# HGRN scores from 32 stationary columns at a time, with masked copies once per head

## The chip, the cores and the metric

The kernel runs on one core of one Trainium2 chip. The metric is the device time of one execution in microseconds, and the time of a kernel is the median of its timed runs. Before the change three runs took 2264.58, 2264.91 and 2265.63 us, so the time before is 2264.91 us.

## The reference, cut to what matters

One decoder layer over 1024 tokens of width 1024, all in float32: a combined input projection, an HGRN2 branch and a retention branch, gates, an output projection and an MLP. The change touches only the scores of the HGRN2 branch, which has 8 heads with 128 keys each:

```python
b = jnp.cumsum(lfc, axis=2)                                   # log of the forget gates
rel = jnp.where(causal, b[:, :, :, None, :] - b[:, :, None, :, :], -jnp.inf)
scores = jnp.einsum('bhid,bhijd,bhjd->bhij', qc, jnp.exp(rel), kc)
o = (jnp.einsum('bhij,bhje->bhie', scores, vc)
     + jnp.einsum('bhid,bhde->bhie', qc * jnp.exp(b), state))
```

The score of query i and key j in a chunk carries, for each of the 128 key channels, the product of the forget gates between j and i. It is not one matrix product. The reference uses chunks of 64 tokens; the result does not depend on their length, and the kernel uses chunks of 128, so a head has 8 chunks.

## The kernel before, in words

The projections and the MLP are dense products of three float32r passes each (`mm3`, lines 188 to 190; the products into the PSUM tiles `psd` are most of them). The HGRN branch lies in the middle of the program. `h_stream` walks over the heads in steps, 9 per head: a step gives one piece of `h_levels` (the scores of head h) and one of `h_states` (the recurrence over the chunks of head h - 1), and `mix` puts dense products (`h_fill`, later `r_first`) between the steps. A scheduler then fixes the order of each engine's instructions when the kernel is built. Every engine runs its own in that order.

`h_levels` makes the scores by doubling. On the first level, tokens stand in pairs (lines 850 to 858). Then `H_SIZES` gives three levels, blocks of 2, 8 and 32 tokens, and each joins four blocks into one of four times the size. Before a level, VectorE (DVE) multiplies the queries `X` and keys `k` by the gates that lie between (lines 880 and 881 before the products, 909, 910, 920 and 921 after them). Then for each of the 8 chunks one product is made whose stationary operand is all 128 keys of the chunk and whose moving operand is 192 query columns (line 891, line 854 on the first level): 128 x 192 results, two chunks to a PSUM bank `psa`. Only those in which key and query lie in the same group of four blocks mean anything. DVE picks them out with `copy_predicated` and byte masks, three copies to a bank (line 906; two on the first level, lines 857 and 858), into the score tile `S` (`hS`, named U in the trace). For the last two heads, ScalarE (ACT) copies the level of 32 in place of DVE (line 899). Float32 products run as two passes, so each is two weight loads and two matmuls in the trace. There are two `psa` buffers.

`h_states` then multiplies `S` by the values (line 957), the decayed queries by the state (956), and the keys by the values (962); it also transposes keys (939) and results (990).

Of the kernel before, what the change touches and what calls it, by code (L numbers as in the profile page):

```python
# [19 lines left out]
P = 128  # L20
# [27 lines left out]
N_MASK = P + 64 + 3 * 384  # L48
# [16 lines left out]
def constants():  # L65
# [15 lines left out]
    m[:, :P] = np.eye(P, dtype=np.float32)  # L81
    r = np.arange(64)[None, :]
    m[:, P:P + 64] = (j % 2 == 0) & (j // 2 == r)
    for n, s in enumerate(H_SIZES):
        half, quad = j // s % 4, j // (4 * s) == r // (2 * s)
        for i, f in enumerate((r // s % 2 * 2, 1, 0)):
            o = P + 64 + 384 * n + 128 * i
            m[:, o:o + 64] = m[:, o + 64:o + 128] = (half == f) & quad
# [46 lines left out]
class Trunk:  # L135
# [703 lines left out]
    def h_levels(self, p, hd):  # L839
# [4 lines left out]
        S = [self.hS[(2 * h + hf) % len(self.hS)] for hf in (0, 1)]  # L844
# [5 lines left out]
        for bk in range(4):  # L850
            pa = self.ps("a", (P, 384)).rearrange("p (c b w) -> p c b w", c=2, w=3)
            for c in (0, 1):
                n = 2 * bk + c
                nc.tensor.matmul(pa[:, c].rearrange("p b w -> p w b"), k[:, n * P:(n + 1) * P], q[:, :, n * 64:(n + 1) * 64], start=True, stop=True)
            Sv = S[bk // 2][:, bk % 2 * 2:bk % 2 * 2 + 2, :].rearrange("p c (b two) -> p c b two", two=2)
            mk = self.mask8[:, :P].rearrange("p (b two) -> p b two", two=2).unsqueeze(1).to_broadcast([P, 2, 64, 2])
            V.copy_predicated(Sv, mk, pa[:, :, :, 0:2])
            V.copy_predicated(Sv[:, :, :, 1], self.mask8[:, P:P + 64].unsqueeze(1).to_broadcast([P, 2, 64]), pa[:, :, :, 2])
            if bk == 1:
                yield  # L860
# [10 lines left out]
        for ln, sz in enumerate(H_SIZES):  # L871
# [14 lines left out]
            for bk in range(4):  # L886
                pa = self.ps("a", (P, 384))
                for c in (0, 1):
                    n = 2 * bk + c
                    mv = X[:, :, n * P:(n + 1) * P].rearrange("p w (b r) -> p b w r", r=4 * sz)[:, :, :, sz:]  # L890
                    nc.tensor.matmul(pa[:, c * 192:(c + 1) * 192].rearrange("p (b w r) -> p b w r", w=2, r=3 * sz),  # L891
                                     k[:, n * P:(n + 1) * P], mv, start=True, stop=True)
                pv = pa.rearrange("p (b w r s) -> p b w r s", w=2, r=3, s=sz)
                Sv = S[bk // 2][:, bk % 2 * 2:bk % 2 * 2 + 2, :].rearrange("p c (b f s) -> p (c b) f s", f=4, s=sz)
                if sz == 32 and p == 3:
                    qv = pv.rearrange("p b w r s -> p b (w r) s")
                    for r0, dst, src in ((0, slice(1, 2), slice(0, 1)), (64, slice(3, 4), slice(2, 3)), (32, slice(2, 4), slice(1, 5, 3)),
                                         (0, slice(2, 4), slice(3, 6, 2))):
                        nc.scalar.activation(Sv[r0:r0 + 32, :, dst], qv[r0:r0 + 32, :, src], AF.Copy)
                    if bk == 1:  # L900
                        yield
                    continue
                for j, (dst, src) in enumerate(((Sv[:, :, 1::2], pv[:, :, 0, 0::2]), (Sv[:, :, 2:4], pv[:, :, :, 1]),
                                                (Sv[:, :, 2:4], pv[:, :, 1, 0::2]))):
                    o = P + 64 + 384 * ln + 128 * j
                    V.copy_predicated(dst, self.mask8[:, o:o + 128].rearrange("p (b two s) -> p b two s", two=2, s=sz), src)
                if bk == 1:
                    yield
# [932 lines left out]
```

## Time and profile before

| what | value |
|---|---|
| median of 3 runs | 2264.91 us |
| profiled execution, its own time | 2266.02 us |
| its span | 2264.2 us |
| TensorE (PE) busy | 98% of the span, 10343 matmuls |
| DVE, ACT, POOL busy | 73%, 45%, 13% |
| first to last score product (lines 854, 891) | 891.5 to 1180.4 us |

PE is the weight loads (PEld) and the matmuls of TensorE; they overlap. A group's row gives busy time, the mean of one in ns and the idle time before it. Matmuls are pipelined: their recorded lengths overlap, so the time from one start to the next is what one costs in a stream. A row of the timeline holds a run of like instructions: its start, its length to the end of the last, and their count.

### The profile page before, as it was taken

The numbers are of one execution on the slowest core, as the hardware profiler recorded it, in microseconds if no ns is written. First come the engines' busy times: TensorE is split into PE (matmuls) and PEld (weight loads), VectorE is DVE, ScalarE is ACT, GpSimd is POOL, SyncE is SP. The second block draws the span as 40 slices with busy tenths as digits, with TensorE's granted clock in tenths as the row PEclk, the third lists the DMA queues.
The fourth block names the chain that finished last, engine by engine and source line by source line (L and its number), as shares of the span: only waits on it lengthen the run. The fifth ranks groups of instructions, "written<-read, shape, count | busy, mean of one in ns | idle before, by whom it ended". The sixth has DMA issues, their size and how long they took to land.

```text
span 2264.2 us, 29883 instructions
## 1 busy us (share of the span) xinstructions
PE 2227.3 (98%) x10343; PEld 1846.9 (82%) x10343; DVE 1645.1 (73%) x3035; ACT 1027.0 (45%) x1889; POOL 299.7 (13%) x469
## 2 busy tenths in 40 slices
PE   7999999999999999999999999999999999999998
PEld 5888888888888887888887888888878888888886
DVE  7866768786777647888875666777796666667778
ACT  4533334543333445343456555222575555643441
POOL 0111111111110112000011222022112222100001
PEclk9999999999999999999999999999999999999999
DMA  9766755543333446121235666864244444777863
GB/s 268 237 220 232 240 184 178 172 144 113 107 114 106 135 172 228 38 85 66 70 127 201 221 215 217 289 213 149 96 162 157 154 154 154 277 267 245 259 217 117
DMA packets 229144, 396.14 MB, mean 175 GB/s; under 512 B 17768, under 2 KB 122976, under 8 KB 228224
## 3 DMA queue, kind: packets, MB, share of 16 engines
q1 hardware_dynamic: 198240, 294.34, 40.5%
q0 software_dynamic: 30576, 99.82, 11.8%
q8 instruction: 82, 1.34, 0.2%
q14 instruction: 70, 0.57, 0.1%
q10 hardware_dynamic: 176, 0.06, 0.0%
HBM read 289.28 MB, written 104.87 MB: 174 GB/s over the span
## 4 chain that ended last, share of the span: by engine, by line
PE 92%; DVE 2%; DMA 2%; issue 2%; ACT 1%; POOL 1%; SPq 0%; DVEq 0%; ACTq 0%; POOLq 0%
PE psd L188 17%; PE psd L189 17%; PE psd L190 17%; PE psa L188 5%; PE psa L189 5%; PE psa L190 5%; PE psc L189 3%; PE psc L188 3%; PE psc L190 3%; PE psa L891 2%; PE psb L1213 2%; PE psb L188 2%; PE psb L189 2%; PE psb L190 2%; PE psc L1199 1%
## 5 line engine op out<-in xcount | busy, mean ns | idle before, releaser
L188 PE MATMUL psd<-U,wh 128*128 128x512 f32 x696 | 280.5, 405 | 1.0 <-ACT U L183 0.9
L189 PE MATMUL psd<-U,wh 128*128 128x512 f32 x696 | 278.4, 400 | 0.5 <-DVE U L184 0.4
L190 PE MATMUL psd<-U,wl 128*128 128x512 f32 x696 | 277.0, 398 | 0.0
L183 ACT ACTIVATE bh<-s 128x512 fp32r<-128x512 f32 x212 | 133.3, 633 | 255.8 <-PE psd L189 65.7
L188 PE MATMUL psd<-U,bh 128*128 128x512 f32 x528 | 205.5, 389 | 1.2 <-DVE e L450 1.2
L189 PE MATMUL psd<-U,bh 128*128 128x512 f32 x528 | 205.6, 389 | 0.1
L190 PE MATMUL psd<-U,bl 128*128 128x512 f32 x528 | 205.5, 389 | 0.0
L183 ACT ACTIVATE bh<-raw 128x512 fp32r<-128x512 f32 x159 | 101.0, 637 | 223.4 <-PE psd L189 92.4
L184 DVE TENSOR_TENSOR bl<-raw,bh 128x512 fp32r<-128x512 f32 x159 | 108.6, 690 | 122.7 <-ACT bh L183 122.3
L184 DVE TENSOR_TENSOR bl<-s,bh 128x512 fp32r<-128x512 f32 x212 | 145.0, 688 | 63.8 <-ACT bh L183 63.7
L189 PEld LDWEIGHTS psd<-U,wh 128*128 128x128 f32 x696 | 132.1, 190 | 26.6 <-DVE U L184 2.7
L188 PEld LDWEIGHTS psd<-U,wh 128*128 128x128 f32 x696 | 131.3, 190 | 27.0 <-ACT U L183 3.4
L190 PEld LDWEIGHTS psd<-U,wl 128*128 128x128 f32 x696 | 131.8, 189 | 25.3
L183 ACT ACTIVATE U<-hr 128x512 fp32r<-128x512 f32 x112 | 70.4, 630 | 143.3 <-issue 71.1
L188 PEld LDWEIGHTS psd<-U,bh 128*128 128x128 f32 x528 | 99.1, 188 | 22.6 <-DVE e L450 2.0
L189 PEld LDWEIGHTS psd<-U,bh 128*128 128x128 f32 x528 | 99.1, 188 | 21.1 <-DVE U L184 0.5
L190 PEld LDWEIGHTS psd<-U,bl 128*128 128x128 f32 x528 | 99.1, 188 | 20.4
L184 DVE TENSOR_TENSOR U<-hr,U 128x512 fp32r<-128x512 f32 x112 | 77.2, 689 | 49.6 <-ACT U L183 49.4
L183 ACT ACTIVATE wh<-raw 128x512 fp32r<-128x512 f32 (+1 forms) x79 | 57.0, 741 | 117.3 <-PE psd L189 88.5
L188 PE MATMUL psa<-U,bh 128*128 128x512 f32 x264 | 103.0, 390 | 1.6 <-ACT e L438 1.6
L190 PE MATMUL psa<-U,bl 128*128 128x512 f32 x264 | 102.7, 389 | 0.0
L189 PE MATMUL psa<-U,bh 128*128 128x512 f32 x264 | 102.7, 389 | 0.0
(447 smaller groups left out, 5593.3 us busy)
## 6 DMA issues: line engine op xcount, KB each, us to landing
raw<-in_w_in SPq DMA_DIRECT2D x146, 512.0 KB
raw<-in_w_down SPq DMA_DIRECT2D x64, 512.0 KB
raw<-in_w_ada SPq DMA_DIRECT2D x32, 512.0 KB
raw<-in_w_up SPq DMA_DIRECT2D x32, 512.0 KB
raw<-in_w_pb SPq DMA_DIRECT2D x20, 512.0 KB
adw<-in_w_ada SPq DMA_DIRECT2D x16, 512.0 KB
v_d<-e POOLq DMA_DIRECT2D x32, 256.0 KB, 4.1
rg_d<-e POOLq DMA_DIRECT2D x32, 256.0 KB, 2.6
```

Of the source, the lines that this page charges most:

```text
L183: self.nc.scalar.activation(hi, src, AF.Copy)
L184: self.nc.vector.tensor_tensor(lo, src, hi.bitcast(F32), op=ALU.subtract)
L188: r = mm(out, wh, uh, start=start, stop=False, skip_group_check=more)
L189: mm(out, wh, ul, start=False, stop=False, skip_group_check=more)
L190: return r, mm(out, wl, uh, start=False, stop=stop, skip_group_check=more)
L891: nc.tensor.matmul(pa[:, c * 192:(c + 1) * 192].rearrange("p (b w r) -> p b w r", w=2, r=3 * sz), k[:, n * P:(n + 1) * P], mv, start=True, ...
L1199: mm(G[e], l[:, n % 2, es], r, start=n == 0 and i == 0, stop=i == 2, skip_group_check=n > 0)
L1213: mm(po, l, r, start=i == 0, stop=i == len(pairs) - 1)
```

## The change

Each chunk's keys are taken in four groups of 32, and each group is multiplied only with the queries of its own 32 tokens. The product of group r goes to PSUM partitions 32r to 32r + 31, at the same columns as the other three. A chunk then gives 4 products of 32 stationary and 48 moving columns for each of the first three levels, in place of one of 128 and 192. The results of all 8 chunks fit in one PSUM bank of 128 x 384, so there are two masked copies on the first level and three on the levels of 2 and 8, per head. They go to a compact tile `hC` of 128 x 256 in which partition 32r + j holds the 32 x 32 diagonal block of key group r for every chunk.

On the level of 32 nothing need be masked, for the four blocks are the four groups. A chunk has four products, of 32, 64, 32 and 64 moving columns. ACT copies the results from two banks straight into `S` (6 copies per head) and then the four diagonal blocks out of `hC` (4 copies), for every head, so line 906's copies of that level go. `S` becomes one tile per head with all 8 chunks, two in turn. The masks are smaller, `rs` shares a tile with `ms`, and a level's products come in one step and not in two.

In numbers of the program: 256 score products become 1024, which in the trace are 512 and 2048 weight loads with as many matmuls. DVE's masked copies fall from 328 to 64. ACT's copies for the scores rise from 32 to 80.

The diff:

```diff
-N_MASK = P + 64 + 3 * 384
+N_MASK = 3 * P + 2 * 384
...
-        S = [self.hS[(2 * h + hf) % len(self.hS)] for hf in (0, 1)]
+        S, C = self.hS[h % 2], self.hC
...
-        for bk in range(4):
-            pa = self.ps("a", (P, 384)).rearrange("p (c b w) -> p c b w", c=2, w=3)
-            for c in (0, 1):
-                n = 2 * bk + c
-                nc.tensor.matmul(pa[:, c].rearrange("p b w -> p w b"), k[:, n * P:(n + 1) * P], q[:, :, n * 64:(n + 1) * 64], start=True, stop=True)
-            ...
-            V.copy_predicated(Sv, mk, pa[:, :, :, 0:2])
-            V.copy_predicated(Sv[:, :, :, 1], self.mask8[:, P:P + 64].unsqueeze(1).to_broadcast([P, 2, 64]), pa[:, :, :, 2])
-            if bk == 1:
-                yield
+        def blocks():
+            pa = self.ps("a", (P, 384))
+            for n in range(8):
+                for r in range(4):
+                    yield n, r, k[:, n * P + 32 * r:n * P + 32 * r + 32], pa[32 * r:32 * r + 32, 48 * n:48 * n + 48], pa
+
+        for n, r, kb, po, pa in blocks():
+            o = n * 64 + 16 * r
+            nc.tensor.matmul(po.rearrange("p (b w) -> p w b", w=3), kb, q[:, :, o:o + 16], start=True, stop=True)
+        pv = pa.rearrange("p (b w) -> p b w", w=3)
+        Cv = C.rearrange("p (b two) -> p b two", two=2)
+        V.copy_predicated(Cv, self.mask8[:, :2 * P].rearrange("p (b two) -> p b two", two=2), pv[:, :, 0:2])
+        V.copy_predicated(Cv[:, :, 1], self.mask8[:, 2 * P:3 * P], pv[:, :, 2])
+        yield
...
-            for bk in range(4):
-                pa = self.ps("a", (P, 384))
-                for c in (0, 1):
-                    ...
-                    nc.tensor.matmul(pa[:, c * 192:(c + 1) * 192].rearrange("p (b w r) -> p b w r", w=2, r=3 * sz),
-                                     k[:, n * P:(n + 1) * P], mv, start=True, stop=True)
-                ...
-                    V.copy_predicated(dst, self.mask8[:, o:o + 128].rearrange("p (b two s) -> p b two s", two=2, s=sz), src)
-                if bk == 1:
-                    yield
+            if last:
+                for hf in (0, 1):
+                    pa = self.ps("a", (P, 384)).rearrange("p (c i) -> p c i", c=4)
+                    for c in range(4):
+                        o = (4 * hf + c) * P
+                        Xc = X[:, :, o:o + P].rearrange("p w (f s) -> p w f s", s=sz)
+                        for r, col, mv in ((0, 0, Xc[:, 0, 1]), (1, 0, Xc[:, :, 2]), (2, 0, Xc[:, 0, 3]), (0, 32, Xc[:, 1, 1::2])):
+                            w = 32 if len(mv.shape) == 2 else 64
+                            po = pa[32 * r:32 * r + 32, c, col:col + w]
+                            nc.tensor.matmul(po if w == 32 else po.rearrange("p (w s) -> p w s", w=2),
+                                             k[:, o + 32 * r:o + 32 * r + 32], mv, start=True, stop=True)
+                    for r in range(3):
+                        w = 96 - 32 * r
+                        nc.scalar.activation(S[32 * r:32 * r + 32, 4 * hf:4 * hf + 4, P - w:], pa[32 * r:32 * r + 32, :, :w], AF.Copy)
+                for r in range(4):
+                    rs = slice(32 * r, 32 * r + 32)
+                    nc.scalar.activation(S[rs, :, rs], C[rs].rearrange("p (c i) -> p c i", c=8), AF.Copy)
+            else:
+                for n, r, kb, po, pa in blocks():
+                    o = n * P + 32 * r
+                    mv = X[:, :, o:o + 32].rearrange("p w (b r) -> p b w r", r=4 * sz)[:, :, :, sz:]
+                    nc.tensor.matmul(po.rearrange("p (b w r) -> p b w r", w=2, r=3 * sz), kb, mv, start=True, stop=True)
+                ...
+                    V.copy_predicated(dst, self.mask8[:, o:o + P].rearrange("p (b two s) -> p b two s", two=2, s=sz), src)
+            yield
...
-                nc.tensor.matmul(po, S[hf][:, c, :], vn, start=n == 0, stop=True)
+                nc.tensor.matmul(po, S[:, n, :], vn, start=n == 0, stop=True)
...
-        k.hS = [X[:, j].rearrange("p (c i) -> p c i", c=4) for j in range(4)]
-        for t in k.hS:
+        k.hS = [X[:, 2 * j:2 * j + 2].rearrange("p a (c i) -> p (a c) i", c=4) for j in (0, 1)]
+        k.hC = k.xp.tile([P, 256], F32, name="hC")
+        for t in k.hS + [k.hC]:
             tc.nc.gpsimd.memset(t, 0.0)
```

The order of PE's instructions at the level of 8 of the second head, before. U_7774 is `X`, fk_7786 is that head's `k`; the rows of L188 to L190 are dense products, L956, L957 and L962 those of `h_states`, and 24 dense rows stand ahead of the first row shown.

```order
L891 MATMUL psa_8266<-U_7774,fk_7786 128x192 x2
L891 MATMUL psa_8272<-U_7774,fk_7786 128x192 x2
L188 MATMUL psd_8292<-U_300,wh_7932 128x512
L189 MATMUL psd_8292<-U_301,wh_7932 128x512
L190 MATMUL psd_8292<-U_300,wl_7933 128x512
L956 MATMUL psc_8320<-st_8264,e_8055 128x128
L957 MATMUL psc_8320<-U_7777,U_7769 128x128
L962 MATMUL psc_8325<-U_7777,e_8174 128x128
L891 MATMUL psa_8329<-U_7774,fk_7786 128x192 x2
L891 MATMUL psa_8335<-U_7774,fk_7786 128x192 x2
L990 MATMUL psb_8351<-cst,e_8109 128x128 x4
```

The same level in the change (L910 is its score product, L966, L967 and L972 are the three of `h_states`):

```order
L190 MATMUL psd_8286<-U_302,wl_7791 128x512
L966 MATMUL psc_8314<-st_8239,e_8113 128x128
L967 MATMUL psc_8314<-U_7777,U_7769 128x128
L972 MATMUL psc_8319<-U_7777,e_8129 128x128
L910 MATMUL psa_8351<-U_7774,fk_7786 32x48 x21
L966 MATMUL psc_8342<-st_8321,e_8114 128x128
L967 MATMUL psc_8342<-U_7777,U_7769 128x128
L910 MATMUL psa_8351<-U_7774,fk_7786 32x48 x10
L972 MATMUL psc_8347<-U_7777,e_8248 128x128
L910 MATMUL psa_8351<-U_7774,fk_7786 32x48
L188 MATMUL psd_8401<-U_296,wh_7959 128x512
```

Two runs of 4 wide products became one of 32 narrow ones, cut in three by products of `h_states`. Over all heads, PE's order has 75 unbroken runs of score products before and 59 in the change, and in both about 24 dense products stand between one level's last product and the next level's first.

On DVE at the same level, before (U_7769 is `S`; D_ are the gates' products):

```order
L906 COPY_PREDICATED U_7769<-mask_315,psa_8329 128x16x8
L906 COPY_PREDICATED U_7769<-mask_315,psa_8335 128x16x8
L906 COPY_PREDICATED U_7769<-mask_315,psa_8329 128x8x16
L906 COPY_PREDICATED U_7769<-mask_315,psa_8335 128x8x16
L906 COPY_PREDICATED U_7769<-mask_315,psa_8329 128x8x16
L906 COPY_PREDICATED U_7769<-mask_315,psa_8335 128x8x16
L909 TENSOR_TENSOR fk_7786<-fk_7786,D_8153 128x2x32x8
L920 TENSOR_TENSOR U_7774<-U_7774,D_8153 128x32x8
L910 TENSOR_TENSOR fk_7786<-fk_7786,D_8244 128x2x32x8
L921 TENSOR_TENSOR U_7774<-U_7774,D_8244 128x2x32x8
```

and in the change (L916 is the masked copy; L918, L919, L929, L930, L883 and L884 answer to L909, L910, L920, L921, L880 and L881 of before):

```order
L916 COPY_PREDICATED hC<-mask_315,psa_8351 128x16x8
L918 TENSOR_TENSOR fk_7786<-fk_7786,D_8227 128x2x32x8
L916 COPY_PREDICATED hC<-mask_315,psa_8351 128x8x16
L184 TENSOR_TENSOR wl_8396<-raw_7542,wh_8395 128x512
L916 COPY_PREDICATED hC<-mask_315,psa_8351 128x8x16
L919 TENSOR_TENSOR fk_7786<-fk_7786,D_8329 128x2x32x8
L929 TENSOR_TENSOR U_7774<-U_7774,D_8227 128x32x8
L930 TENSOR_TENSOR U_7774<-U_7774,D_8329 128x2x32x8
L871 TENSOR_TENSOR hq_7775<-fk_8138 128x512
L883 TENSOR_TENSOR U_7774<-U_7774,D_8330 128x8x32
L886 TENSOR_TENSOR D_8670<-hq_7775 128x2x128
L884 TENSOR_TENSOR U_7774<-U_7774,D_8330 128x2x8x32
```

The second half's six copies, and six more ahead of them, became three; a weight split (L184) and a product for the next head (L871) now stand inside the row of gate products.

More of the change, by code (lines that the diff above doesn't have):

```diff
@@ L80, in constants @@
     m = np.zeros((P, N_MASK), np.uint8)
[L81 to L85, printed above, removed]
+    r = np.arange(P)[None, :]
+    m[:, :2 * P] = j % 32 == np.arange(2 * P)[None, :] % 32
+    m[:, 2 * P:3 * P] = (j % 2 == 0) & (j % 32 // 2 == r % 16)
+    for n, s in enumerate(H_SIZES[:2]):
+        half, quad = j // s % 4, j % 32 // (4 * s) == r // (2 * s) % (8 // s)
         for i, f in enumerate((r // s % 2 * 2, 1, 0)):
-            o = P + 64 + 384 * n + 128 * i
-            m[:, o:o + 64] = m[:, o + 64:o + 128] = (half == f) & quad
+            o = 3 * P + 384 * n + P * i
+            m[:, o:o + P] = (half == f) & quad
     return c, m
@@ L848, in h_levels @@
         yield
-        for bk in range(4):
-            pa = self.ps("a", (P, 384)).rearrange("p (c b w) -> p c b w", c=2, w=3)
-            for c in (0, 1):
-                n = 2 * bk + c
[L854 to L858, printed above, removed]
-            if bk == 1:
-                yield
+        def blocks():
[11 more added lines that the diff above has]
+        yield
         X = self.hX
@@ L885, in h_levels @@
             yield
-            for bk in range(4):
-                pa = self.ps("a", (P, 384))
-                for c in (0, 1):
-                    n = 2 * bk + c
-                    mv = X[:, :, n * P:(n + 1) * P].rearrange("p w (b r) -> p b w r", r=4 * sz)[:, :, :, sz:]
-                    nc.tensor.matmul(pa[:, c * 192:(c + 1) * 192].rearrange("p (b w r) -> p b w r", w=2, r=3 * sz),
-                                     k[:, n * P:(n + 1) * P], mv, start=True, stop=True)
-                pv = pa.rearrange("p (b w r s) -> p b w r s", w=2, r=3, s=sz)
[L894 to L899, printed above, removed]
-                    if bk == 1:
-                        yield
[L902 to L908, printed above, removed]
@@ new lines, in h_levels @@
+            if last:
[20 more added lines that the diff above has]
+                    nc.tensor.matmul(po.rearrange("p (b w r) -> p b w r", w=2, r=3 * sz), kb, mv, start=True, stop=True)
+                pv = pa.rearrange("p (b w r s) -> p b w r s", w=2, r=3, s=sz)
+                Cv = C.rearrange("p (b f s) -> p b f s", f=4, s=sz)
+                for j, (dst, src) in enumerate(((Cv[:, :, 1::2], pv[:, :, 0, 0::2]), (Cv[:, :, 2:4], pv[:, :, :, 1]),
+                                                (Cv[:, :, 2:4], pv[:, :, 1, 0::2]))):
+                    o = 3 * P + 384 * ln + P * j
+                    V.copy_predicated(dst, self.mask8[:, o:o + P].rearrange("p (b two s) -> p b two s", two=2, s=sz), src)
@@ L949, in h_states @@
             ob, sq = (self.e2().rearrange("p (c e) -> p c e", c=4) for _ in (0, 1))
-            ms = self.xp.tile([P, 4], F32, tag="ms", bufs=2, name=self.uid("ms"))
+            mr = self.xp.tile([P, 8], F32, tag="ms", bufs=2, name=self.uid("ms"))
+            ms, rs = mr[:, :4], mr[:, 4:]
             for c in range(4):
@@ L972, in h_states @@
                     nc.vector.tensor_scalar(ms, ms, 1.0 / P, HEAD_EPS, op0=ALU.mult, op1=ALU.add)
-                    rs = self.xp.tile([P, 4], F32, tag="rs", bufs=2, name=self.uid("rs"))
                     nc.gpsimd.tensor_tensor(rs, ms, self.mhalf[:, :4], op=ALU.pow)
```

## The prediction

> **What bounds the kernel now.** I read the page first, then the stage that holds the score products by windows, then its groups, then the chain of waits inside it.
>
> ```profile
> PE 2227.3 (98%) x10343; PEld 1846.9 (82%) x10343; DVE 1645.1 (73%) x3035; ACT 1027.0 (45%) x1889; POOL 299.7 (13%) x469
> PE 92%; DVE 2%; DMA 2%; issue 2%; ACT 1%; POOL 1%; SPq 0%; DVEq 0%; ACTq 0%; POOLq 0%
> ...
> core 0: us, PE busy (x) PEld busy (x) DVE busy (x) ACT busy (x) POOL busy (x), PEclk, DMA share, GB/s
> 886.00:1195.00 309.00, 307.09 (x1710) 269.32 (x1709) 255.20 (x698) 131.79 (x398) 32.61 (x43) 1.00 0.29 98
> ```
>
> TensorE bounds the whole kernel and this stage most of all: 307.1 of 309 us at full clock. DVE is the next, at 255 of 309. So a us taken from DVE alone is worth nothing unless PE waits for DVE, and a us of PE's stream is worth a us. What counts is what the score products cost PE in a stream. The groups of the stage from 890 to 1200 us:
>
> ```profile
> L891 PE MATMUL psa<-U,fk 128*128 128x192 f32 x384 | 72.5, 329 | 1.0 <-ACT U L899 0.8
> L906 DVE COPY_PREDICATED U<-mask,psa 128x128 f32<-128x128 uint8 x264 | 70.2, 316 | 16.1 <-PE psa L891 13.9
> L891 PEld LDWEIGHTS psa<-U,fk 128*128 128x128 f32 x384 | 62.4, 189 | 7.8 <-ACT U L899 2.3 <-issue 2.2 <-PE psc L962 0.3
> L854 PE MATMUL psa<-hq,fk 128*128 128x192 f32 x128 | 24.7, 327 | 0.0
> L857 DVE COPY_PREDICATED U<-mask,psa 128x256 f32<-128x256 uint8 x32 | 13.4, 447 | 0.5 <-PE psa L854 0.3
> L858 DVE COPY_PREDICATED U<-mask,psa 128x128 f32<-128x128 uint8 x32 | 12.5, 462 | 0.0
> L899 ACT ACTIVATE U<-psa 32x64 f32<-32x64 f32 (+1 forms) x32 | 7.4, 237 | 0.4 <-PE psa L891 0.2
> L820 ACT ACTIVATE fk<-psd 128x512 f32<-128x512 f32 x12 | 7.1, 588 | 25.8 <-PE psd L190 25.8
> ```
>
> The 329 ns is one pass from dispatch to its modelled end. In a stream it costs less, which the chain of waits between 915 and 930 us and a second piece of it at 925 show:
>
> ```profile
> 918.27 0.23 PE psd L190
> 918.49 1.30 PE psa L891 x8
> ...
> 925.37 0.44 PE psb L939 x4
> ```
>
> Eight passes take 1.30 us, 0.1625 each; four of 128 columns take 0.44, 0.11 each. A straight line through the two is 5 ns plus 0.82 ns per moving column. A dense pass is 0.23, and 918.27 + 0.23 is 918.50: going from dense to score products costs nothing now when the data are there.
>
> **What is removed on PE.** 384 + 128 = 512 passes at 0.1625 us: 83.2 us, all of it on the path.
>
> **What is added on PE.** 2048 passes: 768 products of 48 columns (1536 passes), 128 of 32 (256) and 128 of 64 (256). No row shows products of different column blocks in flight together, so the cost has two ends.
>
> The upper end is the pace of the columns. If one product runs at a time, the line gives 44 ns for 48 columns, 31 for 32, 57 for 64: 1536 x 44 + 256 x 31 + 256 x 57 = 67.6 + 7.9 + 14.6 = 90 us. The number of columns streamed is the same as before, only the fixed 5 ns come four times as often.
>
> The lower end is the pace of the weight loads. For it there are rows of products with one moving column, where nothing but the load is left, and of loads of one stationary column:
>
> ```profile
> 305.05 0.41 PEld L608 LDWEIGHTS psa<-small,acc 128*128 128x128 f32 x3
> ...
> L1276 PEld LDWEIGHTS psa<-acc,small x16: 80/83/84, 148.1 to 228.5; 128*1 128x1 f32 x16
> ```
>
> Three loads of 128 columns take 0.41 us, the last of them 0.19 by its own length, so (0.41 - 0.19) / 2 = 0.11 from start to start; a quarter is 27.5 ns. The lengths agree: 189 ns for 128 columns less 83 for one is 106 for 127, or 27 for 32. So a load's time goes with its columns. At 27.5 ns all 2048 passes are 56 us; the 64-column products, whose two passes use the same block one after the other, I put at 40 ns, which makes 1792 x 27.5 + 256 x 40 = 59.5 us.
>
> I take the lower end, 60 us. The four products of a chunk use different weights, different PSUM partitions and different columns of the array, so nothing in the rows makes one wait for another but the loads, which share one path. It is the choice on which the forecast stands, and the weakest step. No run here shows such overlap; the Trainium skill, TensorE: Matmul & The Clock Gate, Part 3, says that products of 32 stationary columns put at PSUM partitions 32j run side by side.
>
> **What switching costs.** One kind of narrow product exists before: line 1276, with one stationary column, between dense ones.
>
> ```profile
> 147.82 0.39 PE L190 MATMUL psb<-bh,U 128*128 128x512 f32 x1
> 148.14 1.02 PE L1276 MATMUL psa<-acc,small 128*1 128x256 f32 x4
> 149.09 0.50 PE L188 MATMUL psc<-bh,U 128*128 128x512 f32 x1
> 149.52 0.38 PE L1276 MATMUL psa<-acc,small 128*1 128x256 f32 x1
> ```
>
> The dense pass at 147.82 is through at 148.05, but the narrow run starts at 148.14: 0.09 lost. The run's four passes, at (1.02 - 0.38) / 3 = 0.213 apart, are through at 148.99, and the next dense pass starts at 149.09 with its weight load not begun ahead: 0.10 lost and 0.11 of load exposed. The single dense pass between two narrow runs takes 0.43 in place of 0.23, which is the same 0.20 again. So a run of narrow products costs 0.09 + 0.21, and 0.03 for its own first load: 0.33 us. The change's order has 59 such runs: 19 us, against nothing now. If 32 columns do not behave as one does, it is 0; I take 19, the only row there is.
>
> **Waits.** Score loads now stand idle 7.8 us in all before they start, some of it for semaphores; a level asks for one bank in place of four. I credit 3 us, between 0 and 7.8.
>
> **Off the path.** DVE loses 70.2 + 13.4 + 12.5 = 96 us and gets 8 x 447 + 8 x 462 + 48 x 316 ns = 22 us. The 74 us are worth nothing by themselves, PE being busy throughout. What could matter is the chain from a level's last product to the next level's first:
>
> ```profile
> 945.59 1.47 PE L891 MATMUL psa<-U,fk 128*128 128x192 f32 x8
> 952.56 1.47 PE L891 MATMUL psa<-U,fk 128*128 128x192 f32 x8
> ...
> 946.68 1.51 DVE L906 COPY_PREDICATED U<-mask,psa 128x128 f32<-128x128 uint8 x6
> 948.09 0.69 DVE L909 TENSOR_TENSOR fk<-fk,D 128x512 f32<-128x512 f32 x1
> 951.42 0.69 DVE L881 TENSOR_TENSOR U<-U,D 128x512 f32<-128x512 f32 x1
> ```
>
> From 948.09 to 952.11 the gate products take 4.0 us, and PE comes at 952.56. In the change three copies (0.9) and the two strangers of its order (0.69 each) go with them: 6.3 us, covered by 24 dense passes (5.5), three of the recurrence (0.67) and four transposes (0.44), 6.6 in all. It holds with 0.3 us to spare; each us by which it fails costs up to 24 us over 24 such places. ACT gets 48 copies out of PSUM, between 237 and 588 ns each, and 32 out of SBUF, for 32 of 237: about 24 us more on an engine busy 132 of 309. Per head that is ten copies, some 4 us, behind which line 957's first product waits; 24 dense passes cover it. Without that cover it would be up to 8 x 4 = 32 us. The smaller masks, the memsets and `rs` in the tile of `ms` are hidden behind earlier work.
>
> **The sum.** -83 + 60 + 19 - 3 = -7 us on the profiled execution's 2266.0. The median of the runs is 1.1 below that execution, so 2258 us. Slower decides at a pass time of (83 + 3 - 19) / 2048 = 33 ns: below it the change gains, above it loses.
>
> **Rivals.**
>
> *The blocks take turns* (0.30). Nothing in the trace shows two products together, and every stream in it goes by one product's columns at a time. Then -83 + 90 + 19 - 3 = +23: 2288 us, slower. For it: the nearest stream, L891's own. Against it: the four blocks share no operand but the moving path.
>
> *No price at the switch* (0.15). The drain belongs to line 1276's single column, or to its own waits. Then -83 + 60 - 3 = -26: 2239 us. For it: L939 and L956 beside dense products cost nothing. Against it: two narrow runs in the fence lose the same 0.20.
>
> *Half an overlap* (0.13). A product's two passes share a block, and only the second stands beside the next product's first. A product then costs one load and one pass, 27 + 44 = 71 ns, or 36 per pass: 73 us, and -83 + 73 + 19 - 3 = +6: 2271 us.
>
> *The pace of issue* (0.05). The trace bounds it:
>
> ```profile
> L891 PEldq EVENT_SEMAPHORE  x1: 51/51/51, 1131.6 to 1131.6; - x1
> L956 PEldq EVENT_SEMAPHORE  x1: 51/51/51, 1131.9 to 1131.9; - x1
> 1131.74 1.54 PE L891 MATMUL psa<-U,fk 128*128 128x192 f32 x8
> ```
>
> The sequencer passed the wait of L956 at 1131.9, 0.3 us after that of L891, with the 16 loads and matmuls of eight passes between them in its order: about 0.02 us each, or 0.04 for a pair. At 50 ns a pass, -83 + 102 + 19 - 3 = +35: 2300 us. The Trainium skill, TensorE: Matmul & The Clock Gate, "Wait — 56ns, not 53.3ns?", has the sequencer spend about 62 ns on a matmul when decoding in software; by that page the passes would be 127 us and the time about 2325 us, and these rows speak against it.
>
> The forecast has 0.37.
>
> **How the numbers follow.** A measurement of this kernel tells 0.2%, about 4.5 us, from no change. Forecast: three quarters of its 0.37 is faster, a fifth the same. No price at the switch: faster. Half an overlap: half the same, most of the rest slower. Turns and issue: slower. Faster 0.28 + 0.15 + 0.02 = 0.45, same 0.07 + 0.07 = 0.14 and a little, 0.16, slower 0.39. The range runs from just below the rival without a switch price to just past the one with turns: 2235 to 2291. The forecast's own is 2245 to 2268: the switch between half and all of its price, 0 to 7.8 us of waits, and 56 to 65 us of passes.
>
> **What would show it.** In the changed kernel's timeline a run of 32 products of 48 columns, 64 passes, should start and end within 64 x 27.5 ns = 1.8 us and its tail; near 2.8 means turns, near 2.3 half an overlap, over 3.2 issue. The dense pass behind such a run should start 0.2 us late. The score products' place, 891 to 1180 us, should shrink by about 7 us with PE still busy throughout and DVE down to some 180 of 309. The prediction is wrong if the passes are not 27 to 30 ns apart, if the runs cost no switch, or if PE stands idle for DVE or ACT between levels.

## The result and the profile after

Before, in the runs beside it, 2265.27 us (2264.58 to 2266.01); the changed kernel 2235.05 us (2232.18 to 2239.21). The ratio is 0.986, with an interval of 0.9848 to 0.9873: 30 us faster, where 7 were forecast. The profiled execution took 2232.8 us, its span 2230.9. One run of a later kernel (the one with DVE's copies five times over) took 3678 us at a granted clock of 0.56 and is left out of its time.

The page of the changed kernel, its totals and its chain of waits by engine, then the windows of the stage (busy time of each engine, then the granted clock, the DMA share and GB/s):

```profile
PE 2188.0 (98%) x11879; PEld 1798.4 (81%) x11879; DVE 1579.0 (71%) x2771; ACT 1046.3 (47%) x1937; POOL 302.7 (14%) x468
...
PE 87%; DVE 4%; issue 3%; DMA 2%; ACT 2%; POOL 1%; SPq 0%; DVEq 0%; ACTq 0%; POOLq 0%
...
886.00:1195.00 309.00, 299.51 (x3398) 246.81 (x3397) 204.84 (x460) 170.51 (x489) 42.86 (x54) 0.99 0.34 114
```

PE is still the bound, but it now idles 9.5 of 309 us where before it idled 1.9, and its share of the chain went from 92% to 87%. The clock column reads 0.99 where it read 1.00. Each of the two traces grants half the clock for one stretch of 3.4 us late in the stage, at 1191 us in the change and at 1224 before, which is outside this window; such a stretch costs 1.7 us at most, half its length, and both kernels have one, so nothing of the gain in this stage is clock. (Before's trace has two more of them, at 33 and 47 us; the two profiled spans differ by 33.3 us and the stage by 30.3.) DVE and ACT are busy 204.8 and 170.5 us here, where some 180 and 156 were forecast, but the windows of the two kernels do not hold the same work: the changed kernel has got further by 1195 us. Between the same two dense products (the stretch used for the sum below) DVE falls by 65 us, from 291.6 to 226.2, and ACT rises by 20, from 170.7 to 190.7; 74 and 24 were forecast.

The groups of the changed kernel's stage, 880 to 1170 us, that answer to those of before:

```profile
L910 PE MATMUL psa<-U,fk 128*32 128x48 f32 x1024 | 17.3, 208 | 0.3 <-DVE U L884 0.3
L898 PE MATMUL psa<-U,fk 128*32 128x64 f32 (+1 forms) x512 | 15.6, 213 | 0.4 <-DVE U L930 0.4
L858 PE MATMUL psa<-hq,fk 128*32 128x48 f32 x512 | 7.9, 208 | 0.0
L910 PEld LDWEIGHTS psa<-U,fk 128*32 128x32 f32 x1024 | 13.5, 110 | 4.8 <-issue 1.5 <-DVE U L884 0.5 <-DVE st L977 0.4
L916 DVE COPY_PREDICATED hC<-mask,psa 128x128 f32<-128x128 uint8 x48 | 15.1, 314 | 3.1 <-PE psa L910 3.0
L902 ACT ACTIVATE U<-psa 32x384 f32<-32x384 f32 (+2 forms) x48 | 18.0, 374 | 8.9 <-PE psa L898 8.3
L905 ACT ACTIVATE U<-hC 32x256 f32<-32x256 f32 x32 | 13.2, 411 | 2.9 <-DVE hC L916 2.6
```

The first row holds the surprise: 1024 passes of 208 ns each are busy for 17.3 us together. They must lie on top of each other, about twelve deep by these lengths. So do the loads: 1024 of 110 ns in 13.5 us. The timeline of PE shows one level's products, 64 passes, between dense ones; behind it stand the weight loads of the same place:

```profile
893.62 0.39 PE L190 MATMUL psd<-U,wl 128*128 128x512 f32 x1
893.94 0.89 PE L910 MATMUL psa<-U,fk 128*32 128x48 f32 x64
894.76 0.50 PE L188 MATMUL psd<-U,wh 128*128 128x512 f32 x1
...
893.94 0.75 PEld L910 LDWEIGHTS psa<-U,fk 128*32 128x32 f32 x64 [0.35 <-issue]
894.75 0.19 PEld L188 LDWEIGHTS psd<-U,wh 128*128 128x128 f32 x1
```

The 64 passes take 0.89 us. Less the last one's own 0.208 they start within 0.681 us: 10.8 ns from pass to pass, or some 43 ns for four, which is what one pass of 48 columns costs alone (44 by the prediction's line). Four column blocks run at once, loads and products alike. Ahead and behind, the prediction's switch is there: the dense pass at 893.62 is through at 893.85 and the run starts at 893.94, 0.09 later; the last narrow pass starts at 893.94 + 0.681 = 894.62 and the dense load at 894.75, and the dense pass reads 0.50 long in place of 0.39: 0.11 in which its load lies open.

The level of 32 has products of 32 and 64 columns, three blocks in four, and block 0 gets 96 columns of each chunk:

```profile
1074.74 1.59 PE L898 MATMUL psa<-U,fk 128*32 128x32 f32 x64
```

Less a last pass of 0.22 that is 1.37 us for 64 passes, 21.7 ns each, 171 for a chunk's eight. Two passes of 32 and two of 64 columns by the line are 31 + 31 + 57 + 57 = 176 ns: the fullest block sets the pace.

PE's new idle time lies elsewhere, at the recurrence. Its rows before and after, in the two stages (L956, L962 and L990 of before are L966, L972 and L999 of the change):

```profile
L956 PE MATMUL psc<-st,e 128*128 128x128 f32 x106 | 20.7, 277 | 0.1
L962 PE MATMUL psc<-U,e 128*128 128x128 f32 x106 | 20.9, 279 | 0.0
L990 PE MATMUL psb<-cst,e 128*128 128x128 f32 x56 | 8.4, 273 | 0.0
```

```profile
L966 PE MATMUL psc<-st,e 128*128 128x128 f32 x110 | 23.2, 293 | 1.4 <-DVE st L977 1.2
L972 PE MATMUL psc<-U,e 128*128 128x128 f32 x111 | 22.7, 285 | 1.4 <-ACT e L950 1.1
L999 PE MATMUL psb<-cst,e 128*128 128x128 f32 x56 | 10.3, 284 | 3.2 <-ACT e L989 3.2
```

From 0.1 to 6.0 us. (Both windows end ahead of the last head's transposes, which wait another 1.6 us in either kernel.) The largest piece of the new idle time, in the changed kernel's timelines of PE, ACT and POOL:

```profile
1116.78 0.89 PE L858 MATMUL psa<-hq,fk 128*32 128x48 f32 x64
1119.35 0.91 PE L999 MATMUL psb<-cst,e 128*128 128x128 f32 x3 [1.68 <-ACT e L989]
...
1118.89 1.28 ACT L989 ACTIVATE e<-e,ms 128x128 f32<-128x128 f32 x4 [1.85 <-POOL ms L983]
...
1116.94 1.92 POOL L983 TENSOR_TENSOR ms<-ms,small 128x4 f32<-128x4 f32 x1 [9.80 <-DVE ms L982]
```

POOL takes a power for the norm of a head's outputs (1.92 us), ACT scales the outputs by it, PE transposes them. In PE's stream a head's first level lies between. It was 16 passes of 0.1625 us before, 2.6 in all, and is 0.89 now; PE comes to the transposes and waits 1.7 us.

**The sum, measured.** Between the same two dense products, one ahead of the stage and one behind, lie 368.7 us before (872.73 to 1241.39) and 338.3 in the change (870.27 to 1208.61): 30.3 us of gain lie in this stage. All other products in it are the same ones, 270.9 us at the pace of their streams. Worked out from the starts of the matmuls:

| us in the stage | before | change | predicted difference | measured difference |
|---|---|---|---|---|
| score passes | 83.2 | 31.1 | -23 | -52.1 |
| switches, 59 runs x 0.29 | 0 | 17.1 | +19 | +17.1 |
| all other gaps and waits of PE | 14.5 | 19.3 | -3 | +4.8 |
| sum | | | -7 | -30.3 |

(The 31.1 are 28.6 from first to last start in the runs, and 59 last passes of 0.0425. The 0.29 is the median over the 59 runs: about 0.09 ahead of a run, 0.09 behind its last pass, and 0.11 for the dense load that then lies open. The last row but one is what remains.)

### The profile page after: what moved, and what is told of

Read it like the earlier page. It is cut to its first block, busy times and chain, and to the rows that moved or that the text cites. A ratio compares the mean times of both kernels' runs of the same rounds, so it can differ in the third digit from the quotient of the medians.

```text
span 2230.9 us, 32691 instructions
## 1 busy us (share of the span) xinstructions
PE 2188.0 (98%) x11879; PEld 1798.4 (81%) x11879; DVE 1579.0 (71%) x2771; ACT 1046.3 (47%) x1937; POOL 302.7 (14%) x468
## 4 chain that ended last, share of the span: by engine, by line
PE 87%; DVE 4%; issue 3%; DMA 2%; ACT 2%; POOL 1%; SPq 0%; DVEq 0%; ACTq 0%; POOLq 0%
PE psd L188 17%; PE psd L189 17%; PE psd L190 17%; PE psa L189 5%; PE psa L190 5%; PE psa L188 5%; PE psc L189 3%; PE psc L188 3%; PE psc L190 3%; PE psb L1222 2%; PE psb L188 2%; PE psb L189 1%; PE psb L190 1%; PE psc L1208 1%; PE psa L1156 1%
## 5 line engine op out<-in xcount | busy, mean ns | idle before, releaser
L188 PE MATMUL psd<-U,wh 128*128 128x512 f32 x696 | 278.7, 403 | 1.1 <-ACT U L183 1.1
L190 PE MATMUL psd<-U,wl 128*128 128x512 f32 x696 | 275.0, 396 | 0.0
L188 PE MATMUL psd<-U,bh 128*128 128x512 f32 x528 | 205.5, 389 | 2.2 <-DVE e L450 2.2
L190 PE MATMUL psd<-U,bl 128*128 128x512 f32 x528 | 205.4, 389 | 0.0
L184 DVE TENSOR_TENSOR bl<-raw,bh 128x512 fp32r<-128x512 f32 x159 | 108.4, 689 | 121.6 <-ACT bh L183 121.0
L184 DVE TENSOR_TENSOR bl<-s,bh 128x512 fp32r<-128x512 f32 x212 | 144.6, 687 | 63.6 <-ACT bh L183 63.6
L188 PEld LDWEIGHTS psd<-U,wh 128*128 128x128 f32 x696 | 131.1, 189 | 28.5 <-ACT U L183 3.4
L190 PEld LDWEIGHTS psd<-U,wl 128*128 128x128 f32 x696 | 131.5, 189 | 26.9
L188 PEld LDWEIGHTS psd<-U,bh 128*128 128x128 f32 x528 | 99.1, 188 | 23.7 <-DVE e L450 3.0
L190 PEld LDWEIGHTS psd<-U,bl 128*128 128x128 f32 x528 | 99.1, 188 | 20.4
L184 DVE TENSOR_TENSOR U<-hr,U 128x512 fp32r<-128x512 f32 x112 | 77.0, 687 | 51.2 <-ACT U L183 50.9
L188 PE MATMUL psa<-U,bh 128*128 128x512 f32 x264 | 102.9, 390 | 0.5 <-ACT e L438 0.5
L190 PE MATMUL psa<-U,bl 128*128 128x512 f32 x264 | 102.7, 389 | 0.0
```

The source lines that it names most:

```text
L184: self.nc.vector.tensor_tensor(lo, src, hi.bitcast(F32), op=ALU.subtract)
L188: r = mm(out, wh, uh, start=start, stop=False, skip_group_check=more)
L190: return r, mm(out, wl, uh, start=False, stop=stop, skip_group_check=more)
```

## The experiments

The time before was 2266.17 us beside the first four runs, 2265.15 beside the next four and 2264.83 beside the last four. Under each, "the stage" is the stretch between the same two dense products as above.

**One block at a time.** The three levels of 48 columns, with the order of the products turned round: eight products that share a column block one after the other, then the next block. Loads, passes, columns, copies and switches are the same in number.

```diff
-            for n in range(8):
-                for r in range(4):
+            for r in range(4):
+                for n in range(8):
```

> The 32 narrow products of each of the first three levels in another order: all eight chunks of key group 0, then all of group 1, and so on, so that neighbours in the stream share a column block. Nothing else changes. Theory 'side by side' (four blocks load and multiply at the same time, which made a pass 10.6 ns in the changed kernel): passes of one block take turns, 42 ns each, and the 1536 passes cost 1536 x (42 - 10.6) = 48 us more, 2283 us; the run of 64 passes takes 2.7 us in place of 0.72. Rival 'cheap by itself' (a narrow pass costs 10 ns whatever its neighbours): 2235 us and 0.7 us per run.

Measured: 2266.3 us, 1.0004 of before [0.9994, 1.0013]. The whole gain is gone. The timeline at the same level:

```profile
898.22 0.39 PE L190 MATMUL psd<-U,wl 128*128 128x512 f32 x1
898.54 2.49 PE L910 MATMUL psa<-U,fk 128*32 128x48 f32 x64
900.96 0.50 PE L188 MATMUL psd<-U,wh 128*128 128x512 f32 x1
```

2.49 us in place of 0.89. Within a block the passes start 42.5 ns apart; at the three changes of block the neighbours overlap, so that the mean is 36. The stage is 369.2 us: 66.3 from first to last start in the runs, up by 37.7, and other waits down from 19.3 to 12.4. So neighbours in one block go in turns, neighbours in different blocks side by side, and that is the whole difference between a gain of 30 us and none. What is left of the change cancels out: against before, the passes still save 14 us (the level of 32 keeps its blocks side by side, and the borders overlap), the switches cost 17, and other waits are 2 less. The direction was as expected. It came out below the expected 2283 us because of the overlap at the changes of block and because the slower stream covers waits again. Its rows of the recurrence from 886 to 1195 us, beside the 1.4, 1.4 and 3.2 of the change:

```profile
L966 PE MATMUL psc<-st,e 128*128 128x128 f32 x104 | 21.9, 292 | 0.1
L972 PE MATMUL psc<-U,e 128*128 128x128 f32 x106 | 21.5, 285 | 0.5 <-ACT e L950 0.5
L999 PE MATMUL psb<-cst,e 128*128 128x128 f32 x56 | 10.2, 283 | 0.9 <-ACT e L989 0.9
```

**Two blocks at a time.**

```diff
-            for n in range(8):
-                for r in range(4):
+            for r, n in ((2 * g + i, n) for g in (0, 1) for n in range(8) for i in (0, 1)):
```

> As the changed kernel, but key groups 0 and 1 alternate through all eight chunks, and then groups 2 and 3. Theory 'side by side': two blocks at a time, 21 ns a pass, 1536 x (21 - 10.6) = 16 us more, 2251 us, 1.4 us per run of 64. Rival 'cheap by itself': 2235 us. A third, that loads alone set the pace and only products overlap: 27 ns, 2260 us.

Measured: 2244.36 us, 0.9916 [0.9896, 0.9935].

```profile
898.96 1.42 PE L910 MATMUL psa<-U,fk 128*32 128x48 f32 x64
900.31 0.50 PE L188 MATMUL psd<-U,wh 128*128 128x512 f32 x1
```

From first to last start 1.215 us, 19.3 ns a pass on the mean. Within either pair of blocks two passes start every 43 ns, 21 a pass; the rest is an overlap at the one change of pair. One, two and four blocks give 42.5, 21 and 10.8: the pace goes with the number of blocks in turn, and no pace of issue or of loads shows down to 10.8. The time lies below the expected 2251 us because the passes take 13.6 us more and not 16, and other waits fall from 19.3 to 15.4.

**The fourth block on the level of 32.** There the fourth product of a chunk used block 0 a second time. Sent to partitions 96 to 127, it has a block of its own; the keys it takes stay the first 32. ACT then copies four strips in place of three.

```diff
-  for r, col, mv in ((0, 0, Xc[:, 0, 1]), (1, 0, Xc[:, :, 2]), (2, 0, Xc[:, 0, 3]), (0, 32, Xc[:, 1, 1::2])):
+  for r, kr, mv in ((0, 0, Xc[:, 0, 1]), (1, 1, Xc[:, :, 2]), (2, 2, Xc[:, 0, 3]), (3, 0, Xc[:, 1, 1::2])):
...
-                     k[:, o + 32 * r:o + 32 * r + 32], mv, start=True, stop=True)
-  for r in range(3):
-      w = 96 - 32 * r
-      nc.scalar.activation(S[32 * r:32 * r + 32, 4 * hf:4 * hf + 4, P - w:], pa[32 * r:32 * r + 32, :, :w], AF.Copy)
+                     k[:, o + 32 * kr:o + 32 * kr + 32], mv, start=True, stop=True)
+  for r, kr, q0, w in ((0, 0, 32, 32), (1, 1, 64, 64), (2, 2, 96, 32), (3, 0, 64, 64)):
+      nc.scalar.activation(S[32 * kr:32 * kr + 32, 4 * hf:4 * hf + 4, q0:q0 + w], pa[32 * r:32 * r + 32, :, :w], AF.Copy)
```

> On the level of 32 the fourth product of a chunk (key group 0, 64 columns) goes to PSUM partitions 96 to 127, the column block that this level leaves empty, in place of group 0's own; ACT makes four copies per half in place of three. Theory 'side by side': a chunk is paced by its fullest block, 96 columns before and 64 now, in the trace some 21 ns a pass before and 14 now: 512 x 7 = 3.6 us less, 2231 us, against ACT's 16 added copies of some 0.3 us off the path. Rival 'the level of 32 is slow because of its wider products or its strided queries': no change, 2235 us.

Measured: 2234.55 us, 0.9865 [0.985, 0.988], no different from the change. Its groups, 880 to 1170 us:

```profile
L898 PE MATMUL psa<-U,fk 128*32 128x64 f32 (+1 forms) x512 | 12.3, 212 | 0.4 <-DVE U L929 0.4
L971 PE MATMUL psc<-U,e 128*128 128x128 f32 x106 | 21.6, 286 | 3.0 <-ACT e L949 2.8
L901 ACT ACTIVATE U<-psa 32x128 f32<-32x128 f32 x64 | 20.6, 322 | 8.6 <-PE psa L898 7.9
```

The runs got shorter as expected, by 3.4 us (28.6 to 25.2), and L898's busy time by 3.3. The profiled stage is only 1.2 us shorter, which the medians cannot tell. L971 (L972 of the change) waits 3.0 us, mostly for ACT, where it waited 1.4, and this trace grants half the clock for two stretches of 3.4 us in the stage where the change's grants it for one, which is up to 1.7 us. Between them they can account for the 2.2 us that did not arrive; their shares are not shown. By itself this run shows no gain from faster products.

**Levels ahead of states.** In each step the piece of the scores goes first and the piece of the recurrence second, so that a level's run lies whole between dense products and is not cut by the recurrence: 41 narrow runs in place of 59.

```diff
             for n in range(H_STEPS):
-                next(states, None)
                 next(levels, None)
+                next(states, None)
```

> In each step the level is issued ahead of the recurrence and not behind it, so that PE's order has 41 unbroken runs of narrow products in place of 59. Theory 'a switch costs 0.3 us' (0.09 in, 0.09 out, 0.11 of load): 18 x 0.29 = 5 us less, 2230 us. Rival: the gaps at the switch stand beside waits that were there anyway, or the recurrence, coming later, makes new waits: 2235 us or more.

Measured: 2232.24 us, 0.9854 [0.9838, 0.9871]. The profiled stage is 333.0 us, 5.3 shorter than the change's, which is what 18 switches of 0.29 make; the medians show 3, and their intervals overlap. By itself this does not settle the price of a switch.

**The change again,** beside the next three.

> The changed kernel itself once more, on the same chip as the next three, so that differences of 0.2% can be read: 2235 us, its stage from 890 us on shorter by 30 us than before.

Measured: 2235.7 us, 0.9872 [0.9859, 0.9886]; its stage is 338.3 us long, as it was the first time.

**The fourth block and levels first together.**

> The fourth block on the level of 32 and the level ahead of the recurrence, together. If the two sums held in full: 3.6 + 5 us less than the changed kernel, 2226 us. If what the fourth block saves on the products goes into waits of the recurrence's own products for ACT (its run alone came out at 2234.6 us, with 3 us less of products and as much more of waits): as the level-first kernel alone, 2232 us.

Measured: 2228.53 us, 0.984 [0.9827, 0.9854], 7.2 below the change beside it. The stage is 330.5 us, 7.8 shorter, and its other waits are 21.3, against 20.4 with levels first alone and 19.3 in the change. The time lies between the two that were expected: most of both sums arrives, and some of it goes into waits.

**The same with the outputs taken later.** `H_DEFER` says after how many steps a head's outputs are scaled by ACT (line 989, which waits for POOL's power), and after how many more PE transposes them (999). The first pair holds for heads 0 to 6.

```diff
-H_DEFER = ((1, 2), (2, 3))
+H_DEFER = ((2, 2), (2, 3))
```

> As the one before, and the scaling and transposing of the recurrence's results (ACT's scale behind POOL's power, then four transposes on PE) is put off by one step more for heads 0 to 6. In the trace of the changed kernel PE stands idle 4.8 us of the stage's 9.5 just before these transposes, waiting for ACT. Theory 'the recurrence's output is what PE now waits for': 3 to 5 us less than the kernel beside it. Rival 'the wait moves to the next product in line': no change.

Measured: 2223.2 us, 0.9818 [0.9804, 0.9831]. This beats both kernels: 42 us under before, 12.5 under the change. Its windows and groups (L998 is the transpose, L965 the state's product):

```profile
886.00:1155.00 269.00, 263.96 (x3267) 217.66 (x3265) 189.98 (x437) 157.34 (x467) 40.66 (x44) 1.00 0.33 111
...
L998 PE MATMUL psb<-cst,e 128*128 128x128 f32 x60 | 9.2, 273 | 0.0
L965 PE MATMUL psc<-st,e 128*128 128x128 f32 x112 | 24.1, 297 | 2.8 <-ACT e L967 1.9 <-DVE st L976 0.3 <-DVE st L974 0.3
```

PE idles 5.0 of 269 us, where the change beside it idles 7.6 (its row stands below). The wait of heads 0 to 6 at the transposes is gone (1.8 us in the run before this one, 3.2 in the change), and the stage's other waits are 16.8 in place of 21.3. Up to 1.7 us of that is clock: the run before has one stretch at half clock in the stage, this one none.

**The change with only that constant.**

> The changed kernel with nothing but the scaling and transposing of the recurrence's results put off by one step more. If PE's 4.8 us of idle time before these transposes were lost time: some 4 us less than the changed kernel, 2231 us. If another wait takes their place: 2235 us.

Measured: 2231.87 us, 0.9853 [0.9839, 0.9868], 3 to 4 us below the change.

```profile
L999 PE MATMUL psb<-cst,e 128*128 128x128 f32 x60 | 9.4, 279 | 0.0
```

The row that read 3.2 reads 0.0, and the stage is 333.7 us, 4.6 shorter, with 14.3 of other waits in place of 19.3. Of the 4.8 us of idle time that were expected to go, 1.6 are the last head's, which this constant does not move and which before has too. So the idle time at the outputs of heads 0 to 6 is a cost of the new order's shortness, and can be had back. The intervals of the two times still touch; the rows and the stage carry this, not the medians.

**Later still:** `((2, 3), (2, 3))` with the fourth block and levels first.

> The fastest kernel so far (fourth block, levels first, scaling one step later), with the transposes another step later. If they still waited: up to 1.6 us less, 2222 us. If they no longer set anything: 2223 us.

Measured: 2224.71 us, 0.9818 [0.9804, 0.9833], the same as with `(2, 2)`. What is left does not come from the outputs of heads 0 to 6; the last head's transposes wait 1.6 us in both.

**DVE's copies five times over.** Line 916's copies on the levels of 2 and 8 are each made five times, which gives the same values. It loads DVE again, and was meant to lengthen the chain from a level's products to the next.

```diff
-                    V.copy_predicated(dst, ...)
+                    for _ in range(5):
+                        V.copy_predicated(dst, ...)
```

> The changed kernel with each masked copy of the levels of 2 and 8 made five times over (the result is the same): 192 copies of 0.31 us, 60 us of DVE's work, which is most of what the change took from DVE. Theory 'the chain from products to gate products is just covered': 12 copies of 0.31 us more behind each of 16 runs, 3.7 us on a chain that had 0.3 us to spare, so up to 16 x 3.4 = 54 us, and at least 20, slower than the changed kernel. Rival 'DVE's load does not matter while PE is busy': under 5 us.

Measured: 2237.73 us, 0.9879 [0.9864, 0.9894], 2.0 above the change beside it with overlapping intervals; PE's order has 65 narrow runs here in place of 59. The windows of the change again, then of this kernel (busy PE, PEld, DVE, ACT and POOL):

```profile
886.00:1155.00 269.00, 261.37 (x3196) 215.30 (x3195) 185.66 (x427) 146.16 (x430) 34.41 (x41) 1.00 0.31 105
```

```profile
886.00:1155.00 269.00, 261.53 (x3182) 211.81 (x3181) 224.56 (x614) 143.79 (x420) 33.38 (x40) 1.00 0.32 108
```

DVE is busy 38.9 us more, 83% of the window, the same share as in the kernel before (255 of 309 us), and PE is as busy as without the copies. The lighter DVE is not where the gain came from. On the chain, for which at least 20 us were expected, the run says little. The scheduler put many of the added copies behind the gate products: from a level's last pass to DVE's last product on the queries ahead of the next level the two traces have 4.95 us (the change) and 5.3 (this kernel) on the mean of the 16 places, 0.35 us more and not 3.7.

**A switch measured by itself.** On the order with levels first, one full-width product (a transpose of the identity into the unused quarter of the bank) is put on the three levels of 48 columns, once ahead of each run and once into its middle. The work is the same; the second has one more narrow run at each of 24 places.

```diff
-            pa = self.ps("a", (P, 384))
+            pf = self.ps("a")
+            pa = pf[:, :384]
             for n in range(8):
                 for r in range(4):
+                    if (n, r) == (0, 0):   # (4, 0) in the second
+                        nc.tensor.transpose(pf[:, 384:512], self.ident, self.ident)
```

> The kernel with the level ahead of the recurrence (41 runs of narrow products), and one float32 product of full width (128 x 128, written to 128 unused columns of the level's own bank) put ahead of each of the 24 runs of the first three levels. It adds 24 x 2 passes of 0.11 us, 5.3 us, and no switch: 2237 us. It is the control of the next.

> The same 24 full-width products, each in the middle of its run, so that there are 65 runs in place of 41. Theory 'a switch between narrow and full-width products costs 0.09 + 0.09 + 0.11 us': 24 x 0.29 = 7 us more than its control. Rival 'the gaps at the switch are the ends of waits or of the tail of the last product': no difference to its control.

Measured: ahead 2236.35 us, 0.9871 [0.9854, 0.9887]; inside 2238.74, 0.9882 [0.9867, 0.9897]. The difference of 2.4 us cannot be told from nothing. The added product is one pass in the trace, not two as expected. One place in each, ahead and then inside:

```profile
897.44 0.39 PE L190 MATMUL psd<-U,wl 128*128 128x512 f32 x1
897.67 0.27 PE L856 MATMUL psa<-cst 128*128 128x128 f32 x1
897.87 0.89 PE L913 MATMUL psa<-U,fk 128*32 128x48 f32 x64
898.69 0.50 PE L188 MATMUL psd<-U,wh 128*128 128x512 f32 x1
```

```profile
896.98 0.39 PE L190 MATMUL psd<-U,wl 128*128 128x512 f32 x1
897.30 0.55 PE L913 MATMUL psa<-U,fk 128*32 128x48 f32 x32
897.77 0.33 PE L856 MATMUL psa<-cst 128*128 128x128 f32 x1
898.03 0.55 PE L913 MATMUL psa<-U,fk 128*32 128x48 f32 x32
898.51 0.50 PE L188 MATMUL psd<-U,wh 128*128 128x512 f32 x1
```

The dense passes at 897.44 and 896.98 are through 0.23 later, at 897.67 and 897.21. From there to the next dense pass are 1.02 us in the one and 1.30 in the other, for the same products: 0.28 for the extra run, as the 0.29 above. Over 24 places that should be 6.7 us, yet the two profiled stages are 339.0 and 338.9 long, and the one with fewer runs has 23.6 us of other waits against 15.6. Most of this is the clock. The windows of the two stages, ahead and then inside, have 0.98 and 1.00 in the column of the clock:

```profile
873.40:1212.36 338.96, 329.28 (x3545) 268.48 (x3544) 224.94 (x497) 192.31 (x521) 54.14 (x66) 0.98 0.37 124
```

```profile
873.08:1211.98 338.90, 331.01 (x3545) 267.45 (x3544) 225.43 (x497) 193.43 (x521) 54.14 (x66) 1.00 0.37 123
```

The first trace grants half the clock for three stretches of 3.4 us in its stage, the second for none. Three times 1.7 is up to 5.1 of the 8.0 us between the waits, and without it the added runs come to about 5 us. The first stage is also 6.0 us longer than that of levels first, which has one such stretch: two more are up to 3.4, and the product itself is 24 x 0.11 = 2.6. So the price stands at its place, and the stages fit it once the clock is allowed for; the times of the runs, which differ by 2.4 us, do not show it by themselves.

## Why the prediction was wrong

**What fails is one choice: the pace of the added passes.** "I take the lower end, 60 us", with loads that "share one path" at 27.5 ns each, was named the weakest step. There is no such path among different column blocks. The row of L910's loads, 1024 of 110 ns in 13.5 us, is 13 ns a load, half of what was taken for the least possible, and the passes are 10.8 ns apart on three levels and about 22 on the level of 32. They measured 31.1 us in place of 60. That is 29 us too much in one term; the switches came out 2 us cheaper as well and the waits 8 dearer, which leaves the error of 23. The row from which the 27.5 came was three loads of all 128 columns; it shows that loads of the same columns follow one another at 0.11 us, and was stretched to loads of different ones. The lower end of a range was taken for the least possible, because the only rows were of full-width products. A bound that held was there in the prediction's own line: 44 ns for 48 columns, by four blocks, is 11. That the measured 2235.05 us is also the lower edge of the range is luck: the edge was set by the rival without a price at the switch.

**The switch** was right: 0.33 a run, worked out from line 1276's single column, against 0.29 measured with 32 columns; 17.1 us against 19. The shape is as told, 0.09 ahead, and behind it a drain and a load that lies open. Thus "No price at the switch", whose 2239 us is almost the measured time, is not what happened: the price was there, and the passes were cheaper by more.

**The waits** had the wrong sign. -3 was credited for one bank in place of four; other gaps and waits of PE grew by 4.8. "What could matter is the chain from a level's last product to the next level's first", with 0.3 us to spare, was looked at, and it held: L910 waits 0.3 us for DVE in all. It was not asked what else the old score products had been covering. They covered POOL's power and ACT's scaling in the recurrence, and its steps on DVE and ACT, and when they shrank by 50 us those came to light: 3.2 us at L999, 1.4 each at L966 and L972. With one block at a time, where the passes are longer again by 38 us, they are 0.9, 0.1 and 0.5; with the outputs a step later L999's is 0.0 up to 1170 us.

**DVE's 74 us are worth nothing by themselves**: right, by the copies five times over, and the kernel with one block at a time, which has all of DVE's relief and no gain, agrees. **ACT's ten copies per head**: covered in the main. L967, the product that needs them (line 957 before), stands idle 0.0 us in the stage. L972 waits 1.1 us for ACT's line 950, and 2.8 with the 16 copies more of the fourth block; nothing is near 32.

**The rivals.** "The blocks take turns", -83 + 90, is what happens if neighbours share a block: 42.5 ns a pass where 44 were reckoned. Only the order of the products decides it. "Half an overlap" said 36 a pass and falls with 10.8. "The pace of issue", 50 ns, falls with it; the 0.04 us for a pair of load and matmul that the prediction read from the trace was an upper bound far above what a pair takes. The 62 ns for a matmul with decoding in software, which the prediction cites from the Trainium skill, TensorE: Matmul & The Clock Gate, "Wait — 56ns, not 53.3ns?", does not set the pace here either. Part 3 of the same page of the Trainium skill has products of 32 columns at PSUM partitions 32j side by side, and the runs agree: 42.5, 21 and 10.8 ns a pass for one, two and four blocks. That sentence stood in the prediction and had no weight in the sum. A rival with the loads side by side too, at the 31 us that the passes took, would have been -83 + 31 + 19 - 3 = -36, and was missing from the list.

**Signs named ahead.** "64 x 27.5 ns = 1.8 us and its tail": 0.89 with it. "The dense pass behind such a run should start 0.2 us late": 0.09 + 0.11, yes. PE "busy throughout": no, 9.5 us idle.

## What to carry to other kernels

Products with few stationary columns cost, in a stream, the columns of the fullest column block: send neighbours to different blocks of 32, in turn, and give each block the same number of columns. Keep such products in long runs, since each run between full-width products costs 0.29 us of PE's stream here, as much as 27 passes. When a stream on the bounding engine shrinks by 50 us, ask of every chain on the other engines that ran beside it whether it is still covered, and move its end a step later if it is not; here that, longer runs and the fourth block were worth another 12 us. And read the granted clock of a stage before you compare it with another: here one stretch of 3.4 us at half clock, present in one trace and absent in the next, is as large as some of the effects.

## What the runs showed of the hardware that was not expected

Weight loads of different column blocks go together, though every product here uses all 128 rows of the array: 64 loads, each 0.110 us long, start and end within 0.75 us. Part 3 of TensorE: Matmul & The Clock Gate, in the Trainium skill, says that loads overlap with products in flight only if their row groups differ; the rows here are against it.

The two float32 passes of one product do not hold up the four blocks, and they do not start next to each other. In the program's order one product follows another, and each is two passes. In the run at 893.94 the passes start four at a time: at 0, 6, 13 and 20 ns, then at 67, 73, 80 and 86, and from there on every 43 ns. On the level of 32 the first three starts of the run at 1074.74, at 0, 7 and 13 ns, have 32, 64 and 32 columns, the widths of three products in three blocks. So a pass seems to wait only for the one before it in its own block, while passes of other blocks go ahead of it. The trace does not name the block of a pass; this is read from the starts and the widths.

The borders in the kernel with one block at a time fit that. There 63 x 42.5 ns would be 2.68 us from first to last start; it was 2.49 - 0.21 = 2.28. The 0.40 between them, over three borders, is 0.13 each, three passes: after the thirteenth of a block's sixteen passes another starts 6 ns later, and the block's last three go on at 42.5 ns beside the first of the next.
